# A pooling and short-convolution decoder block on one core: another step order in the first unit, a longer hold and a shorter landing count in the planner, and a rearranged closing normalisation

## The chip, the cores and the metric

The kernel runs on one core of one Trainium2 chip. The metric is the device time of one execution in microseconds (us); of the kernel before it is 2356.65 us, the median of 3 runs (2355.65 to 2356.98). TensorE (PE) multiplies, VectorE (DVE) and ScalarE (ACT) prepare its operands and take its results, SyncE (SP) and GpSimd (POOL) mostly issue DMAs.

## What is computed

One decoder block on x of shape (256, 4096), float32:

```python
h = rmsnorm(x, norm_w)
u_p, z_p, u_c, b_c, c_c, z_c, g = split(h @ w_in)      # six of width 2048, one of 8192
y_pool = pool(u_p) * silu(z_p)                         # pool: trailing windows, then a small linear map
y_conv = b_c * conv3(c_c * u_c) * silu(z_c)
merged = sigmoid(g_0 + gate_b_0) * (y_pool @ w_branch_0) + sigmoid(g_1 + gate_b_1) * (y_conv @ w_branch_1)
out = rmsnorm(x + merged @ w_out, final_norm_w)
```

The weights w_in (4096 x 20480), w_branch (2 x 2048 x 4096) and w_out (4096 x 4096) are read once each.

## The kernel before, in words

**Units and steps.** The output columns of all products are cut into units of 1024 (`cz0`, `cb0`, ... for w_in, `b0_0` to `b1_3` for w_branch, `o0` to `o3` for w_out). A unit runs through the rows of its weight in steps of 256 rows (16 steps, 8 for a branch), and a step reads one slab of weights of 1 MB into one of three buffers `raw`. A plain step ("P") makes 8 groups of 3 matmuls, since each float32 product is made of three: high times high, high times low and low times high, where "high" is the value rounded to the multiplier's format and "low" the remainder. A step of kind "S" needs only 7 groups (Strassen's scheme), but sums of quarters of both operands.

**Preparation.** For a step ACT rounds the weights (`highs`, line 231) and DVE subtracts (`lows`, line 235); both write into the 15 cells of `ring`, 4 cells for a P step, 7 for an S step. PE gives a cell back after its last product with it, and only then can another step be prepared in it. The left operands (x, later y and merged) stand in `arena` as pairs of high and low.

**The order of work is made at build time.** `pump` (line 988) lays down the preparation of the steps up to four ahead, and issues the load of step j+3 when step j is prepared; `after_group` (line 1032) is called after each group of matmuls, takes the banks that are complete out of PSUM (`evacuate` on ACT) and calls `pump`, unless it is told to hold. In the closing P step of a unit it holds after the groups 3 to 6 (line 1090). Every engine then works through its list in that order.

**The first unit** (`cz0`) has to build the pairs of x while it uses them. It runs all 16 steps as P steps, in the order `FIRST` (line 35). The operands 0 to 7 are plain pairs: ACT scales x by the norm's weight into the high (`x_direct`, line 914), DVE makes the low (`x_low`, line 908). The operands 8 to 15 are "staged": later units use them in S steps, so ACT scales into the buffer `sa` (`x_scale`, line 925) and DVE makes four sums, the rounded copy and the remainder, and copies one pair more into `extra` (`x_sums`, line 931). The staged operand of step j is laid down behind the lows of step j-1. At steps 4, 7, 10 and 13 rows of x are fetched, and at steps 6, 9, 12 and 15 they are squared for the first norm, one half on ACT and one on DVE (lines 887 to 890). The preparation of steps 0 and 1 is made in four pieces, that of the others in one; `halved` steps (line 855) are made in two.

**Fills** (class `Fill`, line 782) refresh the pairs in `arena` for later products: the planner counts ticks, one for every 6 matmuls, and lets a fill go on `LANDING` = 12 ticks after its DMA was issued (line 816). The fills of `merged` (`m_d`) belong to unit `o0`, four operands for each chunk c of 1024 columns.

**The end.** In the last unit, `o3`, three P steps are kept back and run by halves: first both column halves of the token rows 0 to 127 (t = 0), then for t = 1 one column half after the other. After each half `finish_half` (line 1175) adds the bank to `E` on DVE, squares it on ACT with a row sum into `ossq`, and multiplies it by the norm's weight on DVE. `finish` (line 1182) makes the reciprocal root of the mean (`rstd_of`, line 875: a reduction, a scale, the root on ACT, a reciprocal and three small products on DVE), scales four blocks of 128 x 1024 (one on ACT, three on DVE) and writes them out with one DMA each, the ACT block from ACT's queue and the others from SP's.

Of the kernel before, what the change touches and what calls it, by code (L numbers as in the profile page):

```python
# [15 lines left out]
P = 128  # L16
# [15 lines left out]
TAIL = 3  # L32

SIX5 = "PPPPPSPSPSPSPSPS"
FIRST = (0, 1, 8, 2, 9, 3, 10, 11, 4, 12, 13, 5, 14, 6, 15, 7)
OPENED = 12
SEVEN3 = "PPPSPSPSPSPSPSPS"
NINE = "PSPSPSPSSPSPSSPS"
# [12 lines left out]
def hybrid_block(ctx: ExitStack, tc: tile.TileContext, x, xc, prm, rows_in, w_in, pool_w, w_branch, w_out, out):  # L51
# [5 lines left out]
    def act(dst, src, func=AF.Copy, **kw):  # L57
        return pin(nc.scalar.activation(dst, src, func, **kw))  # L58
# [116 lines left out]
    class Operand:  # L175

        def __init__(self, kind, region):
            self.o, room = place(region)
            n = 4 if kind == "P" else room
            self.kind, self.region, self.n = kind, region, n  # L180
            self.ready = False
# [598 lines left out]
        o.ready = True  # L780

    class Fill:
        def __init__(self, o, src, free, ready):
            self.o, self.free, self.ready, self.src = o, free, ready, src
            self.at = self.st = None
            self.phase = self.due = 0

# [25 lines left out]
    def pop_fill(force=None):  # L813
        now[0] += 1
        for f in list(fills):
            if f.at is not None and f.free() and (now[0] >= f.at + LANDING or f.o is force):
                if f.advance(f.o is force):
                    break
        used = [f.st for f in fills if f.at is not None]
        nxt = next((f for f in fills if f.at is None), None)  # L820
        if nxt is None or not nxt.ready() or now[0] < hush[0]:
            return
        st = next((q for q in stages if not any(q is u for u in used)), None)
        if st is not None:
            nxt.fetch(st)
# [27 lines left out]
    steps = [s for u in units for s in u.steps]  # L853
    for a, b in zip(steps, steps[1:]):
        b.halved = a.kind == "S" and b.kind == "P"
    last = units[-1]
    assert all(s.kind == "P" for s in last.steps[-TAIL:])
    tail = last.steps[-TAIL:]
# [13 lines left out]
    for _ in range(WARM):  # L872
        pin(nc.tensor.matmul(shared(3)[:, 0:2 * P], warm[:, 0:P], warm, start=True, stop=True))

    def rstd_of(q, r, name):
        a = q.shape[1]
        m = sb(f"{name}_m", [P, a])
        s = sb(f"{name}_s", [P, a])
        pin(nc.vector.tensor_reduce(out=m, in_=q, axis=mybir.AxisListType.X, op=ALU.add))
        pin(nc.vector.tensor_scalar(out=m, in0=m, scalar1=1.0 / D, scalar2=EPS, op0=ALU.mult, op1=ALU.add))  # L880
        act(s, m, AF.Sqrt)
        pin(nc.vector.reciprocal(out=r, in_=s))
        mul(m, m, r)
        stt(m, m, -0.5, r, ALU.mult, ALU.mult)
        stt(r, m, 1.5, r, ALU.add, ALU.mult)
# [179 lines left out]
    def queue_fills():  # L1065
        for n in range(2):
            for i in [s.op for s in names[f"b{n}_0"].main]:
                j = y_ops[n].index(i)
                fills.append(Fill(i, y_d[n, j // 4][:, j % 4].rearrange("p k t -> p (k t)"), freed(i),
                                  lambda: True))  # L1070
# [104 lines left out]
    def finish_half(t, n):  # L1175
        cs = slice(n * NH, (n + 1) * NH)
        add(E[:, t, cs], PE_[t][n], E[:, t, cs])
        act(sa[:, 4 * n:4 * n + 4].rearrange("p o c -> p (o c)"), E[:, t, cs], AF.Square,
            accum_out=ossq[:, t, 3 + n:4 + n])
        mul(rest[:, t, cs], E[:, t, cs], Y[:, 0, cs])  # L1180

    def finish(t):
        r = rout[:, t:t + 1]
        rstd_of(ossq[:, t:t + 1], r, f"rout{t}")
        for c in range(4):
            v = rest[:, t] if c == 3 else parked[c][:, t]
            if c == 1:
                act(v, v, scale=r)
            else:
                pin(nc.vector.tensor_scalar(out=v, in0=v, scalar1=r, scalar2=None, op0=ALU.mult))  # L1190
        for c in (1, 0, 2, 3):
            v = rest[:, t] if c == 3 else parked[c][:, t]
            queue_ = nc.scalar if c == 1 else nc.sync
            pin(queue_.dma_start(of[t * P:(t + 1) * P, c * NU:(c + 1) * NU], v))

    for t in range(2):
        for ns in ((0, 1),) if t == 0 else ((0,), (1,)):
# [49 lines left out]
```

## Time and profile before

| what | before |
|---|---|
| median of 3 runs | 2356.65 us (2355.65 to 2356.98) |
| profiled execution | 2356.82 us, of which the span is 2354.7 us |
| PE busy | 2340.7 us, 10424 matmuls |
| weight loads of PE busy | 1938.7 us |
| DVE busy | 2217.8 us |
| ACT busy | 1542.9 us |
| POOL busy | 139.0 us |
| HBM read, written | 521.46 MB, 25.17 MB |

The span runs from the first to the last instruction; the rest of the execution's time lies around it. "Busy" is a share of the span. In the rows, "L61" is line 61 of the kernel, the helper that all two-operand DVE operations go through, so the tiles' names tell the operations apart: `ring<-raw,ring` are lows, `ring<-raw` on ACT are highs, `arena<-Y,par` are plain pairs of x, `sa` is the staging buffer. A row of a timeline has the start, the time, the engine, the operation and its count, and in brackets how long the engine was idle before it and what ended the wait.

### The profile page before, as it was taken

What the parts mean: (1) busy time and instruction counts of PE and PEld (TensorE: products, weight loads), DVE (VectorE), ACT (ScalarE), POOL (GpSimd) and SP (SyncE); (2) the same over time, 40 slices, a digit from 0 to 9 for tenths busy, and PEclk for the clock granted to TensorE, in tenths of its full rate; (3) what the DMA queues carried; (4) which work ended last, traced back from release to release, by engine and by line L of the source; (5) the groups of instructions that cost most, each with busy time, mean ns of one, the idle gap of its engine ahead of it and who ended that gap; (6) DMA issues with size and microseconds to landing.
All of it is one profiled execution on the core that took longest, in us unless ns stands there. A gap on an engine that the chain in (4) does not pass through costs nothing.

```text
span 2354.7 us, 28337 instructions
## 1 busy us (share of the span) xinstructions
PE 2340.7 (99%) x10424; PEld 1938.7 (82%) x10424; DVE 2217.8 (94%) x2454; ACT 1542.9 (66%) x1841; POOL 139.0 (6%) x195
## 2 busy tenths in 40 slices
PE   9999999999999999999999999999999999999998
PEld 7888888888888888888888888888888888888886
DVE  8899989999979979979999999998999899999998
ACT  6666756766656666666677767677666566566664
POOL 0000000000001000100000000001101001000000
PEclk9999999999999999999999999999999999999999
DMA  9667655776656656656787787778767678767877
GB/s 351 231 234 248 217 201 215 251 232 233 222 207 216 219 196 213 220 198 222 242 258 254 256 265 246 250 267 283 258 225 247 254 247 282 250 206 263 260 255 279
DMA packets 95387, 569.44 MB, mean 242 GB/s; under 512 B 10320, under 2 KB 10576, under 8 KB 34832
## 3 DMA queue, kind: packets, MB, share of 16 engines
q1 hardware_dynamic: 69824, 485.39, 56.7%
q0 software_dynamic: 24848, 81.01, 13.7%
q8 instruction: 81, 1.33, 0.2%
q10 hardware_dynamic: 576, 1.24, 0.1%
q14 instruction: 58, 0.48, 0.1%
HBM read 521.46 MB, written 25.17 MB: 232 GB/s over the span
## 4 chain that ended last, share of the span: by engine, by line
PE 97%; DVE 1%; DMA 0%; ACT 0%; issue 0%; DVEq 0%; SPq 0%; ACTq 0%
PE sums L1026 70%; PE shared L1026 25%; PE shared L676 1%; PE shared L462 1%; DVE ring L61 1%; DMA raw<-in_w_branch_dram 0%; DVE parts L61 0%; DMA raw<-in_w_in_dram 0%; ACT ring L58 0%; DVE arena L61 0%; PE shared L652 0%; DVE J L61 0%; ACT E L58 0%; PE shared L653 0%; PE shared L655 0%
## 5 line engine op out<-in xcount | busy, mean ns | idle before, releaser
L1026 PE MATMUL sums<-ring,arena 128*128 128x512 f32 x7011 | 1640.7, 390 | 1.9 <-ACT E L58 1.1
L1026 PEld LDWEIGHTS sums<-ring,arena 128*128 128x128 f32 x7011 | 1315.3, 188 | 275.5 <-ACT E L58 1.5
L61 DVE TENSOR_TENSOR ring<-raw,ring 128x1024 fp32r<-128x1024 f32 (+2 forms) x887 | 962.2, 1104 | 70.4 <-ACT ring L58 69.5
L58 ACT ACTIVATE ring<-raw 128x1024 fp32r<-128x1024 f32 (+3 forms) x682 | 785.5, 1192 | 210.2 <-PE sums L1026 98.5
L58 ACT ACTIVATE ring<-parts 128x512 fp32r<-128x512 f32 (+1 forms) x683 | 510.4, 761 | 510.2 <-DVE parts L61 438.3
L1026 PE MATMUL shared<-ring,arena 128*128 128x512 f32 x2241 | 541.1, 389 | 0.0
L61 DVE TENSOR_TENSOR ring<-parts,ring 128x1024 fp32r<-128x1024 f32 (+1 forms) x475 | 524.5, 1146 | 8.7 <-ACT ring L58 8.7
L1026 PEld LDWEIGHTS shared<-ring,arena 128*128 128x128 f32 x2241 | 420.6, 188 | 87.3
L61 DVE TENSOR_TENSOR parts<-parts,raw 128x512 f32<-128x512 f32 x444 | 303.3, 683 | 0.0
L61 DVE TENSOR_TENSOR parts<-raw 128x1024 f32<-128x1024 f32 x222 | 270.2, 1217 | 10.9 <-DMA raw<-in_w_in_dram 6.0
L61 DVE TENSOR_TENSOR J<-J 128x512 f32<-128x512 f32 (+1 forms) x90 | 78.1, 868 | 6.0 <-ACT J L58 2.8
L1026 PE MATMUL sums<-ring,last_pair 128*128 128x512 f32 x306 | 76.2, 389 | 0.0
L58 ACT ACTIVATE J<-shared 128x512 f32<-128x512 f32 x128 | 69.5, 601 | 1.6
L1026 PEld LDWEIGHTS sums<-ring,last_pair 128*128 128x128 f32 x306 | 57.4, 188 | 11.9
L85 POOL DMA_DIRECT2D E<-J x28 | 34.2, 1463 | 479.5 <-ACT ring L58 300.1
L1026 PE MATMUL shared<-ring,last_pair 128*128 128x512 f32 x216 | 51.9, 389 | 0.0
L1026 PE MATMUL shared<-ring,side 128*128 128x512 f32 x207 | 50.7, 389 | 0.0
L1026 PEld LDWEIGHTS shared<-ring,last_pair 128*128 128x128 f32 x216 | 40.5, 188 | 8.4
L1026 PEld LDWEIGHTS shared<-ring,side 128*128 128x128 f32 x207 | 38.9, 188 | 8.1
L58 ACT ACTIVATE E<-sums 128x512 f32<-128x512 f32 x76 | 41.8, 592 | 4.5 <-PE sums L1026 2.7
L85 POOL DMA_DIRECT2D Y<-J x12 | 14.7, 1458 | 265.1 <-ACT ring L58 138.5
L58 ACT ACTIVATE E<-sums,rin 128x512 f32<-128x512 f32 x20 | 13.0, 689 | 13.9 <-PE sums L1026 13.9
(140 smaller groups left out, 645.6 us busy)
## 6 DMA issues: line engine op xcount, KB each, us to landing
raw<-in_w_in_dram SPq DMA_DIRECT2D x318, 1024.0 KB, 4.9
raw<-in_w_branch_dram SPq DMA_DIRECT2D x64, 1024.0 KB, 5.4
raw<-in_w_out_dram SPq DMA_DIRECT2D x64, 1024.0 KB, 4.8
E<-J POOLq DMA_DIRECT2D x28, 512.0 KB, 8.6
E<-in_rows_dram POOLq DMA_DIRECT2D x14, 512.0 KB, 9.8
Y<-J POOLq DMA_DIRECT2D x12, 512.0 KB, 9.3
gates_d<-E POOLq DMA_DIRECT2D x6, 1024.0 KB, 6.1
y_d<-E POOLq DMA_DIRECT2D x8, 512.0 KB, 5.2
```

Of the source, the lines that this page charges most:

```text
L58: return pin(nc.scalar.activation(dst, src, func, **kw))
L61: return pin(nc.vector.tensor_tensor(out=dst, in0=a, in1=b, op=op))
L85: return pin(nc.gpsimd.dma_start(dst, src, accum_op=ALU.add))
L462: pin(nc.tensor.transpose(shared(j)[:, i * T + t * P:i * T + (t + 1) * P], src[:, t, c:c + P], ident))
L676: pin(nc.tensor.matmul(o, a, b, start=(k, i) == (0, 0), stop=(k, i) == (3, 2)))
L1026: pin(nc.tensor.matmul(ps, lhs, rhs, start=n == 0, stop=n == u.total[b] - 1))
```

## The change

Six edits, none of which changes a matmul or the number of matmuls:

```diff
-FIRST = (0, 1, 8, 2, 9, 3, 10, 11, 4, 12, 13, 5, 14, 6, 15, 7)
+FIRST = (0, 1, 2, 3, 8, 4, 9, 5, 10, 11, 12, 13, 14, 6, 15, 7)
...
+    for s in steps[2:5]:
+        s.halved = True
...
-            if f.at is not None and f.free() and (now[0] >= f.at + LANDING or f.o is force):
+            if f.at is not None and f.free() and (now[0] >= f.at + f.landing or f.o is force):
...
-                              lambda c=c: c in merged and now[0] >= merged[c]))
+                              lambda c=c: c in merged and now[0] >= merged[c], LANDING // (1 + c // 3)))
...
-            after_group(u, g[0], st, st is u.steps[-1] and st.kind == "P" and 3 <= i < len(gs) - 1)
+            after_group(u, g[0], st, st is u.steps[-1] and st.kind == "P" and (0 if u is names["b0_0"] else 3) <= i < len(gs) - 1)
...
+    def mean_of(q, m):
+        pin(nc.vector.tensor_reduce(out=m, in_=q, axis=mybir.AxisListType.X, op=ALU.add))
+        pin(nc.vector.tensor_scalar(out=m, in0=m, scalar1=1.0 / D, scalar2=EPS, op0=ALU.mult, op1=ALU.add))
...
+        if n == 0:
+            mean_of(ossq[:, t:t + 1, 0:4], known[:, t:t + 1])
         mul(rest[:, t, cs], E[:, t, cs], Y[:, 0, cs])
...
     def finish(t):
-        r = rout[:, t:t + 1]
-        rstd_of(ossq[:, t:t + 1], r, f"rout{t}")
-        for c in range(4):
-            v = rest[:, t] if c == 3 else parked[c][:, t]
+        r, last_, k = rout[:, t:t + 1], ossq[:, t, 4:5], known[:, t:t + 1]
+        act(dev[:, t:t + 1], last_, AF.Sqrt, scale=1.0 / D, bias=k)
+        stt(mean[:, t:t + 1], last_, 1.0 / D, k, ALU.mult, ALU.add)
+        refined(mean[:, t:t + 1], dev[:, t:t + 1], r)
+        pieces = []
+        for c, a, n in ((0, 0, NH), (1, 0, NH), (0, NH, NH), (1, NH, NH), (2, 0, NU), (3, 0, NU)):
+            v = (rest[:, t] if c == 3 else parked[c][:, t])[:, a:a + n]
             if c == 1:
                 act(v, v, scale=r)
             else:
                 pin(nc.vector.tensor_scalar(out=v, in0=v, scalar1=r, scalar2=None, op0=ALU.mult))
-        for c in (1, 0, 2, 3):
-            v = rest[:, t] if c == 3 else parked[c][:, t]
+            pieces.append((c, a, n, v))
+        for c, a, n, v in pieces:
             queue_ = nc.scalar if c == 1 else nc.sync
-            pin(queue_.dma_start(of[t * P:(t + 1) * P, c * NU:(c + 1) * NU], v))
+            pin(queue_.dma_start(of[t * P:(t + 1) * P, c * NU + a:c * NU + a + n], v))
```

In words: the first unit takes the plain operands 0 to 3 first and has five staged ones in a row at steps 8 to 12; its steps 2 to 4 are prepared in two halves. In the closing step of `b0_0` the planner lays down no preparation between any of the groups. The last four fills of `merged` (c = 3) wait 6 ticks instead of 12. At the end, the mean over the first four row sums is taken when the first half is squared, the root takes the last sum as a term of its own, and the first two blocks are scaled and written in halves.

Three places of the built program, as the engines' lists stand. First DVE in the first unit, from the lows of step 1 on (`ring<-raw,ring`), with the low of a plain pair (`arena<-Y,par,arena`, line 73) and the making of a staged operand (the rows with `sa`). Before:

```order
L61 TENSOR_TENSOR ring<-raw,ring 128x512 x4
L61 TENSOR_TENSOR sa<-sa 128x128 x4
L774 CAST arena<-sa 128x896
L61 TENSOR_TENSOR arena<-sa,arena 128x896
L774 CAST extra<-sa 128x128
L61 TENSOR_TENSOR extra<-sa,extra 128x128
L61 TENSOR_TENSOR ring<-raw,ring 128x4x512
L73 SCALAR_TENSOR_TENSOR arena<-Y,par,arena 128x256 x2
L61 TENSOR_TENSOR ring<-raw,ring 128x3x512
L61 TENSOR_TENSOR ring<-raw,ring 128x512
```

The same stretch of DVE's list in the change:

```order
L61 TENSOR_TENSOR ring<-raw,ring 128x512 x4
L73 SCALAR_TENSOR_TENSOR arena<-Y,par,arena 128x256 x2
L61 TENSOR_TENSOR ring<-raw,ring 128x2x512 x2
L73 SCALAR_TENSOR_TENSOR arena<-Y,par,arena 128x256 x2
L61 TENSOR_TENSOR ring<-raw,ring 128x2x512
L61 TENSOR_TENSOR ring<-raw,ring 128x512 x2
L61 TENSOR_TENSOR sa<-sa 128x128 x4
L774 CAST arena<-sa 128x896
L61 TENSOR_TENSOR arena<-sa,arena 128x896
L774 CAST extra<-sa 128x128
L61 TENSOR_TENSOR extra<-sa,extra 128x128
L61 TENSOR_TENSOR ring<-raw,ring 128x2x512 x2
```

The staged operand 8 has moved behind the lows of the steps 2 and 3, and plain pairs stand in its place.

Second DVE at the end of the program, from the adding of the first half of t = 1 (`sums_83` is its bank, `sums_84` that of the second half; the products into `parts` are those with the norm's weight). Before:

```order
L61 TENSOR_TENSOR E<-sums_83,E 128x512
L61 TENSOR_TENSOR parts<-E,Y 128x512
L61 TENSOR_TENSOR E<-sums_84,E 128x512
L61 TENSOR_TENSOR parts<-E,Y 128x512
L879 TENSOR_REDUCE rout_m<-ossq 128x1
L880 TENSOR_SCALAR rout_m<-rout_m 128x1
L882 RECIPROCAL rout<-rout_s 128x1
L61 TENSOR_TENSOR rout_m<-rout_m,rout 128x1
L73 SCALAR_TENSOR_TENSOR rout_m<-rout_m,rout 128x1
L73 SCALAR_TENSOR_TENSOR rout<-rout_m,rout 128x1
L1190 TENSOR_SCALAR raw<-raw,rout 128x1024 x2
L1190 TENSOR_SCALAR parts<-parts,rout 128x1024
```

The same place of DVE's list in the change:

```order
L61 TENSOR_TENSOR E<-sums_83,E 128x512
L878 TENSOR_REDUCE rout_k<-ossq 128x1
L879 TENSOR_SCALAR rout_k<-rout_k 128x1
L61 TENSOR_TENSOR parts<-E,Y 128x512
L61 TENSOR_TENSOR E<-sums_84,E 128x512
L61 TENSOR_TENSOR parts<-E,Y 128x512
L73 SCALAR_TENSOR_TENSOR rout_m<-ossq,rout_k 128x1
L890 RECIPROCAL rout<-rout_s 128x1
L61 TENSOR_TENSOR rout_m<-rout_m,rout 128x1
L73 SCALAR_TENSOR_TENSOR rout_m<-rout_m,rout 128x1
L73 SCALAR_TENSOR_TENSOR rout<-rout_m,rout 128x1
L1205 TENSOR_SCALAR raw<-raw,rout 128x512 x2
```

The reduction and its scale stand behind the first add now, ahead of the product with the norm's weight; they read `ossq`, which ACT writes from that add. The same two rows stand at that place for t = 0. Behind these rows follow one scale of `raw` (128x1024) and one of `parts` in the change.

Third ACT at the end of `b0_0`, where it copies the corner banks (`J<-shared`), rounds the next unit's weights (`ring<-raw`), makes the high of a fill (`arena<-sb`) and takes out the four product banks (`E<-sums`). Before:

```order
L58 ACTIVATE J<-shared_88 128x512
L58 ACTIVATE ring<-raw 128x3x512
L58 ACTIVATE arena<-sb 128x512
L58 ACTIVATE E<-sums_82 128x512
L58 ACTIVATE E<-sums_84 128x512
L58 ACTIVATE E<-sums_81 128x512
L58 ACTIVATE E<-sums_83 128x512
```

In the change ACT's list has the same rows in the same order at this place, and so have the other engines' lists; nothing moved there.

More of the change, by code (lines that the diff above doesn't have):

```diff
@@ L782, in hybrid_block, with __init__ @@
     class Fill:
-        def __init__(self, o, src, free, ready):
-            self.o, self.free, self.ready, self.src = o, free, ready, src
+        def __init__(self, o, src, free, ready, landing):
+            self.o, self.free, self.ready, self.src, self.landing = o, free, ready, src, landing
             self.at = self.st = None
@@ L878, in rstd_of, with refined @@
         s = sb(f"{name}_s", [P, a])
-        pin(nc.vector.tensor_reduce(out=m, in_=q, axis=mybir.AxisListType.X, op=ALU.add))
-        pin(nc.vector.tensor_scalar(out=m, in0=m, scalar1=1.0 / D, scalar2=EPS, op0=ALU.mult, op1=ALU.add))
+        mean_of(q, m)
         act(s, m, AF.Sqrt)
+        refined(m, s, r)
+    def refined(m, s, r):
         pin(nc.vector.reciprocal(out=r, in_=s))
@@ L1069, in queue_fills @@
                 fills.append(Fill(i, y_d[n, j // 4][:, j % 4].rearrange("p k t -> p (k t)"), freed(i),
-                                  lambda: True))
+                                  lambda: True, LANDING))
         for o in [s.op for s in names["o0"].main]:
@@ L1179, in finish_half @@
             accum_out=ossq[:, t, 3 + n:4 + n])
+        if n == 0:
+            mean_of(ossq[:, t:t + 1, 0:4], known[:, t:t + 1])
         mul(rest[:, t, cs], E[:, t, cs], Y[:, 0, cs])
+    known, mean, dev = (sb(f"rout_{k}", [P, 2]) for k in "kms")
     def finish(t):
-        r = rout[:, t:t + 1]
-        rstd_of(ossq[:, t:t + 1], r, f"rout{t}")
-        for c in range(4):
-            v = rest[:, t] if c == 3 else parked[c][:, t]
+        r, last_, k = rout[:, t:t + 1], ossq[:, t, 4:5], known[:, t:t + 1]
[5 more added lines that the diff above has]
+            v = (rest[:, t] if c == 3 else parked[c][:, t])[:, a:a + n]
             if c == 1:
```

## The prediction

> **What bounds the kernel now.** I start with the page: the span, the busy shares and the chain that ended last.
>
> ```profile
> span 2354.7 us, 28337 instructions
> PE 2340.7 (99%) x10424; PEld 1938.7 (82%) x10424; DVE 2217.8 (94%) x2454; ACT 1542.9 (66%) x1841; POOL 139.0 (6%) x195
> PE 97%; DVE 1%; DMA 0%; ACT 0%; issue 0%; DVEq 0%; SPq 0%; ACTq 0%
> ```
>
> PE is busy for all but 14 us, and its matmuls are the chain. The change leaves every matmul in place, so it can only touch those 14 us, or add to them. Next come the waits of PE, and two pieces of the chain in order of time.
>
> ```profile
> PE shared L873 <- DVE warm L869: 1.1, 1, 1.1
> PE sums L1026 <- ACT E L58: 1.1, 1, 1.1
> PE sums L1026 <- DVE ring L774: 0.8, 1, 0.8
> 5.98 96.11 PE sums L1026 x414
> 2326.72 17.01 PE sums L1026 x75
> ```
>
> Three waits are listed: two before the first real matmul at 5.98, which the change does not touch, and one of 1.1 us on an eviction of ACT. The last row gives 17.01 / 75 = 0.227 us for one matmul, so a P step of 24 takes 5.44 us. The 414 matmuls from 5.98 on take 96.11 us; at 0.227 they would take 94.0, and the 2.1 us more are a slow start (below). Hence there is no room in the first unit behind its start: step j begins at about 13.3 + 5.44 (j - 1). The rest of the 14 us is the end, from the last matmul to 2354.7, about 11 us.
>
> **The first unit: order and halves.** Price: nothing. The rows of before, in the timeline:
>
> ```profile
> 10.33 2.50 DVE L61 TENSOR_TENSOR ring<-raw,ring 128x512 fp32r<-128x512 f32 x4
> 14.50 1.92 ACT L58 ACTIVATE ring<-raw 128x2048 fp32r<-128x2048 f32 x1 [1.50 <-DMA raw<-in_w_in_dram]
> 16.45 2.29 DVE L61 TENSOR_TENSOR ring<-raw,ring 128x2048 fp32r<-128x2048 f32 x1
> 17.65 2.01 ACT L58 ACTIVATE ring<-raw 128x1536 fp32r<-128x1536 f32 x2 [0.44 <-DMA raw<-in_w_in_dram]
> 18.66 0.87 DVE L73 SCALAR_TENSOR_TENSOR arena<-Y,par,arena 128x256 fp32r<-128x256 f32 x2
> 30.10 1.01 DVE L61 TENSOR_TENSOR sa<-sa 128x128 f32<-128x128 f32 x4
> 33.29 1.22 DVE L73 SCALAR_TENSOR_TENSOR E<-E 128x1024 f32<-128x1024 f32 x1
> 64.04 1.92 ACT L58 ACTIVATE ring<-raw 128x2048 fp32r<-128x2048 f32 x1 [2.72 <-PE sums L1026]
> ```
>
> Step 2 (lows at 16.45) is ready at 18.74, and PE comes to it at 18.7: the only tie in the unit, and one that cost nothing. At 64.04 it is ACT that waits for PE to give cells back, so preparation is ahead there. DVE's prices: lows 2.29, a plain low 0.87, a staged operand 33.29 - 30.10 = 3.19, a square 1.2. I carry DVE's list along with them, in the new order. The lows of step 1 end at 12.83, as before. Step 2: the weights are there at 14.50, the highs come in halves of about 0.96 at 15.5 and 16.4, the plain low fits into the wait, and the lows end at 16.7 and 17.85, 0.9 before PE. Step 3: weights at 17.65, lows end at 21.2 (PE 24.2). Step 4: 3.19 of staging and 2.3 of lows, 26.7 (29.6). Steps 5 to 8 end at 29.8, 36.4, 39.6 and 45.1 (PE 35.1, 40.5, 45.9, 51.4). Then the five staged steps in a row, 8 to 12: DVE needs 5 x (3.19 + 2.29) + 2 x 1.2 = 29.8 us for what PE does in 27.2, so the lead falls from 6.3 to 3.5 us at step 12 (ready 69.6, PE 73.1), and grows again. PE never waits: **zero**. The cover is this lead; without it the run costs PE 29.8 - 27.2 = 2.6 us. Below zero there is nothing to gain, as PE has no gap here. The loads keep their order in SP's queue and are issued when the steps are prepared, within about 3 us of before.
>
> **The hold in the closing step of b0_0.** This is the wait of 1.1 us:
>
> ```profile
> 1715.76 1.49 ACT L58 ACTIVATE ring<-raw 128x1536 fp32r<-128x1536 f32 x1 [1.29 <-DMA raw<-in_w_branch_dram]
> 1717.15 0.61 ACT L58 ACTIVATE arena<-sb 128x512 fp32r<-128x512 f32 x1
> 1717.67 2.04 ACT L58 ACTIVATE E<-sums 128x512 f32<-128x512 f32 x4
> 1718.30 6.00 PE L1026 MATMUL sums<-ring,arena 128*128 128x512 f32 x25 [1.07 <-ACT E L58]
> ```
>
> ACT stands behind a load that lands at 1715.76, then rounds three cells and a fill, and only at 1717.67 takes out the first bank, which PE waits for until 1718.30. To gain, the rounding would have to move behind the evictions. The order of ACT shows that it does not: the rows are the same, since that preparation was laid down before the closing step began. So the hold costs and brings **nothing**; if it did what it says, the 1.1 us would go.
>
> **The fills of c = 3.** They move one pair of steps ahead, about 10 us:
>
> ```profile
> 2041.97 0.56 POOL L82 DMA_DIRECT2D sa<-m_d  x1 [4.57 <-DVE parts L61]
> sa<-m_d POOLq DMA_DIRECT2D x8, 256.0 KB, 5.2
> 2052.40 1.49 ACT L58 ACTIVATE ring<-raw 128x1536 fp32r<-128x1536 f32 x1 [3.00 <-PE sums L1026]
> 2061.41 1.02 DVE L61 TENSOR_TENSOR sa<-sa 128x128 f32<-128x128 f32 x4
> ```
>
> The DMA of the first is issued at 2041.97 and lands some 5 us later, at 2047; its sums now stand at 2051.2 instead of 2061.4, so the data is there. Two sums (2.0 us) come ahead of a preparation in whose course ACT waits 3.0 us for PE at 2052.40; DVE's delay of at most 2 to 3 us is inside a lead of a like size, and PE has no wait there to give back: **zero**, at worst some 0.5 us.
>
> **The end.** Here stands the one term that isn't zero. The rows of before:
>
> ```profile
> 2335.60 0.69 DVE L61 TENSOR_TENSOR E<-sums,E 128x512 f32<-128x512 f32 x1 [1.05 <-PE sums L1026]
> 2336.32 0.63 ACT L58 ACTIVATE sa<-E 128x512 f32<-128x512 f32 x1 [7.01 <-DVE E L61]
> 2336.86 0.19 ACT L58 ACTIVATION_READ_ACCUMULATOR sa<-E 128x1 f32 x1
> 2338.41 0.16 DVE L879 TENSOR_REDUCE rout_m<-ossq 128x1 f32<-128x5 f32 x1
> 2339.80 1.42 DVE L1190 TENSOR_SCALAR raw<-raw,rout 128x1024 f32<-128x1024 f32 x2
> 2341.80 0.68 DVE L61 TENSOR_TENSOR E<-sums,E 128x512 f32<-128x512 f32 x1
> 2343.76 0.69 DVE L61 TENSOR_TENSOR E<-sums,E 128x512 f32<-128x512 f32 x1 [0.55 <-PE sums L1026]
> 2345.24 0.16 DVE L879 TENSOR_REDUCE rout_m<-ossq 128x1 f32<-128x5 f32 x1
> 2345.85 0.16 DVE L882 RECIPROCAL rout<-rout_s 128x1 f32<-128x1 f32 x1 [0.27 <-ACT rout_s L58]
> 2346.63 1.42 DVE L1190 TENSOR_SCALAR raw<-raw,rout 128x1024 f32<-128x1024 f32 x2
> 2347.41 0.99 SPq L1194 DMA_DIRECT2D out_dram<-raw  x2
> DMA packets 506, 1.88 MB, mean 417 GB/s; under 512 B 48, under 2 KB 48, under 8 KB 506
> DMA packets 986, 1.36 MB, mean 272 GB/s; under 512 B 233, under 2 KB 469, under 8 KB 986
> ```
>
> The row with 417 GB/s is the stretch 2348.5 to 2353.0: the writes of t = 1 run at one rate from the first DMA (issued 2347.41) to the end, 2.10 MB / 417 = 5.0 us. So **the issue of the first DMA sets the end**. What must be late for it? The first half of t = 1 was complete in PSUM at about 2339.5, but DVE adds it only at 2341.80: DVE is behind, with the scales of t = 0. Then it waits 0.55 us for PE and adds the second half at 2343.76.
>
> The edit shortens the chain behind the second square: the reduction and its scale go (2345.24 to 2345.62, 0.38 us), and the first scale is half as long (about 0.36 for 0.71). But it puts the reduction behind the *first* add, where DVE, whose list is in order, must wait for ACT's square. For t = 0: the add ends at 2336.29, square and sum end at 2337.05, reduction and scale take until 2337.42; the product starts at 2337.44 instead of 2336.32. The second add moves from 2336.93 to 2338.05, the second square ends at 2339.50, the root at 2339.71, the reciprocal starts at 2339.74 and the first scale 0.78 later (2346.63 - 2345.85), at 2340.52 against 2339.80. The four scales are followed by the first add of t = 1 at 2342.54 against 2341.80. There the same wait comes once more: square done at 2343.99, reduction and scale until 2344.36, product, and the second add starts at 2344.99, although its bank was complete at 2343.7. Square done 2346.44, root 2346.65, reciprocal 2346.68, first scale 2347.46 against 2346.63. Its half ends 0.36 later, and the first DMA goes at 2347.90 against 2347.41: **0.5 us later**. Behind it the halves follow each 0.36, and 256 KB take 0.63 us at 417 GB/s, so the writes do not starve.
>
> The halves have rows of 2 KB in place of 4 KB. The trace has no such write. Its nearest rows are loads with 2 KB rows in the first 7 us, a mean of 272 GB/s (last row, the stretch 2 to 7) with pauses; by that the 1.05 MB in halves would take 3.9 us for 2.5, 1.3 more; at 417 GB/s, nothing. I take 0.15, near the lower end, since the slow start of the program is in the 272.
>
> Sum: 0 + 0 + 0 + 0.5 + 0.15 = +0.65 us against the profiled execution, 2356.82 (span 2354.7 and 2.1 around it), 2357.47. The median lies 0.17 below that execution, so I forecast 2357.3 us. Ends: -0.75 (both savings at the end arrive, no backlog) and +1.8 (halves at 272 GB/s).
>
> **The rivals.** *The end is faster.* If DVE were not behind, or the waits for the squares cost it less, the savings of 0.38 and 0.36 remain: 2355.9. For it speaks the shorter chain, against it the add at 2341.80, 2.3 us after its bank. A further 1.1 us would go if the load at 1715.76 landed earlier by chance: 2354.8. *The hold or the order bring more*, over 0.2%: that needs 4.7 us out of the 14, of which 6 lie before the first matmul and 5 are writes; I see no place.
>
> *Slower: the five staged steps starve PE.* The place is step 12, the price 2.6 us if the lead at step 8 is zero instead of 6.3; it decides from a lead under 2.6. A stop of that length could also throw PE back to its slow start, which cost 2.1 us (the 96.11 row). With the end that is 2356.65 + 0.65 + 2.6 + 2.1 = 2362.0. Against it speaks the row at 64.04, where ACT waits for PE.
>
> The wait at 1718.30 bears on the second part of this price: 1.07 us of idle PE, and the 25 matmuls behind it take 6.00 us, 0.24 each, so PE stayed fast. [...]
>
> *The change does nothing at the end either* (the waits and the savings cancel): 2356.6.
>
> **How the numbers follow.** About 0.2% (4.7 us) is what a measurement of this kernel can tell from no change. Forecast, the end later by 0.2 to 1.8 us: 0.62. End unchanged or faster: 0.26. A small starvation of PE, under 4 us: 0.06. The starvation with a slow restart: 0.04. Faster by over 0.2%, for a reason not seen: 0.02. So faster 0.02, same 0.94, slower 0.04. The range takes both ends of the term and what lies in the run of before: 2355.0 to 2359.2.
>
> **What would show it.** In the changed profile PE's waits should again be one on the warm-up, one on `ring` and one of about 1.1 us on `E`; a fourth on `ring` or `arena` between 60 and 80 us would be the starvation. The reduction should stand 0.8 us after the add that it follows, idle for ACT's `sa`, and the second add of t = 1 near 2345.0, without a wait for PE; if it waits for PE again, the backlog was misread and the end is faster. The first write of t = 1 should be issued near 2347.9 and the writes fill 5.0 to 5.3 us.

## The result and the profile after

The changed kernel took **2360.45 us**, the median of 20 runs (2359.53 to 2362.82), against 2356.74 us for 20 runs of the kernel before in the same series (2355.65 to 2359.19). The ratio is 1.0016, with a 95% interval of 1.001 to 1.0023. The forecast was 2357.3 with a range up to 2359.2: the sign was right, the time lies above the range. On the two profiled executions the spans are 2358.7 and 2354.7 us, 4.0 apart.

The page of the changed kernel, span and busy shares:

```profile
span 2358.7 us, 28360 instructions
PE 2344.0 (99%) x10424; PEld 1938.6 (82%) x10424; DVE 2218.6 (94%) x2461; ACT 1544.3 (65%) x1846; POOL 139.0 (6%) x195
```

PE is 3.3 us busier with the same 10424 matmuls. No case of the prediction had that. Its list of waits, which was the first thing to look at by the prediction, is the same as before, with one of them shorter (the columns are the sum, the number and the longest, in us):

```profile
PE shared L875 <- DVE warm L871: 1.1, 1, 1.1
PE sums L1034 <- DVE ring L774: 0.8, 1, 0.8
PE sums L1034 <- ACT E L58: 0.7, 1, 0.7
```

So PE lost its 3.3 us without waiting for anyone: its matmuls themselves are longer. The view that groups PE's instructions by line and tiles says which. Before:

```profile
L1026 PE MATMUL shared<-ring,arena 128*128 128x512 f32 x2241 | 541.1, 389 | 0.0
L1026 PE MATMUL sums<-ring,last_pair 128*128 128x512 f32 x306 | 76.2, 389 | 0.0
L1026 PE MATMUL shared<-ring,last_pair 128*128 128x512 f32 x216 | 51.9, 389 | 0.0
```

The changed kernel, in the same view:

```profile
L1034 PE MATMUL shared<-ring,arena 128*128 128x512 f32 x2241 | 541.1, 389 | 0.0
L1034 PE MATMUL sums<-ring,last_pair 128*128 128x512 f32 x306 | 78.1, 395 | 0.0
L1034 PE MATMUL shared<-ring,last_pair 128*128 128x512 f32 x216 | 53.3, 396 | 0.0
```

Of each row the busy time (in us) and the mean of one (in ns) matter. Matmuls overlap, so the mean of 389 ns, from a matmul's start to its end, is longer than the distance from one start to the next, which is 226.7 ns by the start times. Only the 522 matmuls whose pair comes from `last_pair` have changed: 395 and 396 ns, 233 ns from start to start. They cost (78.1 + 53.3) - (76.2 + 51.9) = **3.3 us** more. Those on `arena` are as before.

The other part is the end. The timeline of the changed kernel from the last matmuls to the first writes:

```profile
2345.09 1.56 PE L1034 MATMUL sums<-ring,last_pair 128*128 128x512 f32 x6
2345.48 0.68 DVE L61 TENSOR_TENSOR E<-sums,E 128x512 f32<-128x512 f32 x1
2346.95 0.16 DVE L878 TENSOR_REDUCE rout_k<-ossq 128x1 f32<-128x4 f32 x1 [0.79 <-ACT sa L58]
2347.82 0.68 DVE L61 TENSOR_TENSOR E<-sums,E 128x512 f32<-128x512 f32 x1
2350.39 1.54 DVE L1205 TENSOR_SCALAR raw<-raw,rout 128x512 f32<-128x512 f32 x3
2350.91 1.39 SPq L1209 DMA_DIRECT2D out_dram<-raw  x3
```

The rows stand where the prediction put them relative to the last matmul: the reduction idles 0.79 us for ACT's `sa`, and the second add comes without a wait for PE. The last matmul ends at 2345.09 + 1.56 = 2346.65, the first write is issued at 2350.91, and the span ends at 2358.7. Set against the last matmul of before, whose row is this,

```profile
2342.20 1.52 PE L1026 MATMUL sums<-ring,last_pair 128*128 128x512 f32 x6
```

the stretches are (times in us; three further kernels of the experiments stand beside them):

| kernel | last matmul to first write | first write to end | together |
|---|---|---|---|
| before | 2343.72 to 2347.41: 3.69 | 7.29 | 10.98 |
| changed | 2346.65 to 2350.91: 4.26 | 7.79 | 12.05 |
| e1, changed kernel at the addresses of before | 2344.55 to 2348.90: 4.35 | 7.60 | 11.95 |
| e12, whole blocks | 2341.70 to 2346.20: 4.50 | 7.30 | 11.80 |
| e7, reduction later | 2341.22 to 2344.38: 3.16 | 7.62 | 10.78 |

The end has cost 1.07 us. The third difference is the wait in the closing step of `b0_0`, 0.71 for 1.07 us. Together 3.3 + 1.07 - 0.36 = 4.0 us, which is the difference of the spans.

### The profile page after: what moved, and what is told of

Its sections match the earlier page's. It is cut to its first block, busy times and chain, and to the rows that moved or that the text cites. A ratio compares the mean times of both kernels' runs of the same rounds, so it can differ in the third digit from the quotient of the medians.

```text
span 2358.7 us, 28360 instructions
## 1 busy us (share of the span) xinstructions
PE 2344.0 (99%) x10424; PEld 1938.6 (82%) x10424; DVE 2218.6 (94%) x2461; ACT 1544.3 (65%) x1846; POOL 139.0 (6%) x195
## 4 chain that ended last, share of the span: by engine, by line
PE 97%; DVE 2%; ACT 0%; DMA 0%; issue 0%; DVEq 0%; SPq 0%; ACTq 0%
PE sums L1034 70%; PE shared L1034 25%; PE shared L676 1%; PE shared L462 1%; DVE ring L61 1%; DMA raw<-in_w_branch_dram 0%; DVE parts L61 0%; ACT ring L58 0%; DMA raw<-in_w_in_dram 0%; DVE arena L61 0%; ACT sa L58 0%; DVE raw L1205 0%; PE shared L652 0%; DVE J L61 0%; DVE E L61 0%
## 5 line engine op out<-in xcount | busy, mean ns | idle before, releaser
L1034 PE MATMUL sums<-ring,arena 128*128 128x512 f32 x7011 | 1640.7, 390 | 1.5 <-DVE ring L774 0.8
L61 DVE TENSOR_TENSOR J<-J 128x512 f32<-128x512 f32 (+1 forms) x90 | 78.1, 868 | 6.3 <-ACT J L58 2.8
L1034 PE MATMUL sums<-ring,last_pair 128*128 128x512 f32 x306 | 78.1, 395 | 0.0
L1034 PE MATMUL shared<-ring,last_pair 128*128 128x512 f32 x216 | 53.3, 396 | 0.0
```

The source lines that it names most:

```text
L61: return pin(nc.vector.tensor_tensor(out=dst, in0=a, in1=b, op=op))
L1034: pin(nc.tensor.matmul(ps, lhs, rhs, start=n == 0, stop=n == u.total[b] - 1))
```

## The experiments

The theory after these traces: six edits that touch no matmul have shifted a tile. The changed kernel keeps three small tiles of [128, 2] (`known`, `mean`, `dev`) where before had four of [128, 1] (two each for t = 0 and t = 1). By the addresses of the built program a tile of either kind takes 32 bytes of each partition, so the pool that holds them is one tile smaller, and `last_pair`, which stands behind it, starts at byte 187424 instead of 187392. `raw`, from which most of the output is written at the end, moves by 32 bytes too, from 195584 to 195616. In the kernel before, all tiles that feed those products start at multiples of 512: `arena` 2560, `ring` 88576, `extra` 171008, `side` 179200, `last_pair` 187392. The rival: the end, the order of the first unit or the small tiles themselves make the difference, and the longer matmuls come with them. In the diffs below, `front` and `back` are tiles that nothing uses; `back` has 40 columns of 4 bytes in both kernels.

**The address alone, from both sides: e1 and e2.** e1 is the changed kernel with its tiles back at the addresses of before.

```diff
-    sb("back", [P, 40])
+    sb("back", [P, 48])
```

> The kernel after, with 32 bytes more of filling in the upper part of the memory, so that every tile there has the address of before (last_pair at 187392 instead of 187424). Nothing else is changed. Theory P (place): the matmuls with last_pair as stationary operand take 6.3 ns more each because the tile starts 32 bytes further on; expected is a pitch of 226.7 ns for them, PE busy 2340.7 us, and 2357.3 us (before 2356.7, plus 1.1 for the end, less 0.4 at the eviction of b0_0). Rival Q (order): the pitch rises because the changed order of the lists lets ACT or DVE touch last_pair or raw at the same time; expected is then still 233 ns and 2360.4 us.

e2 is the kernel before with `last_pair` and `raw` at the addresses of the changed one.

```diff
-    sb("back", [P, 40])
+    sb("back", [P, 32])
```

> The kernel before, with 32 bytes less of filling: the tiles of the upper part start 32 bytes further on, last_pair at 187424. No instruction moves. Theory P: 233 ns for the 521 matmuls with last_pair, PE busy 2344.0 us, 2359.5 us (3.3 us more, of which the waits at b0_0 and in o2 take back 0.4 to 0.6). Rival Q: no change, 2356.7 us.

Measured: e1 2356.66 us, ratio to before 0.9997 (0.9988 to 1.0006); e2 2361.26, ratio 1.0018 (1.0009 to 1.0026), beside 2357.03 for before. PE's group in e1, then in e2:

```profile
L1034 PE MATMUL sums<-ring,last_pair 128*128 128x512 f32 x306 | 76.2, 389 | 0.0
```

```profile
L1026 PE MATMUL sums<-ring,last_pair 128*128 128x512 f32 x306 | 78.1, 395 | 0.0
```

Eight unused columns take the whole loss away from the changed kernel, and eight fewer put 4.2 us on the kernel before, where nothing else was touched. The address is the main cause. The medians give it 3.8 and 4.2 us, more than the 3.3 of the matmuls, and e2 is 1.8 above its expectation. In the traces of before and e2 the last matmul comes 4.3 us later: 3.3 of that in the matmuls on `last_pair`, 0.2 in a later first product, 0.6 among those on `arena`, waits included. The writes of the end, too, take about 0.1 us longer with `raw` 32 or 64 bytes further on: 7.38 us from the first write to the end in e2 and 7.41 in e5, against 7.27 to 7.30 in before, e10, e11 and e12, which write whole blocks with `raw` at the address of before. The rest I can't put down to the address.

**Which distance: e4, e6, e5, e13, e14.** Is it the tile's own address, or its place against the other operand? e4 moves `ring`, the moving operand of nearly all matmuls, and the tiles behind it by 32 bytes, `last_pair` too, but not `arena`:

```diff
+    blocks("gap", [P, 8])
     ring = blocks("ring", [P, CELLS, 2, NH], F32R)
...
-    sb("back", [P, 40])
+    sb("back", [P, 32])
```

> The kernel before with 32 bytes between arena and ring, and 32 bytes less of filling above: arena stays, ring, extra, side and last_pair start 32 bytes further on. If only the stationary operand's place counts: extra (36), side (276) and last_pair (521) take 6.3 ns more each, 5.2 us, 2361.9 us; the matmuls with arena keep 227 ns although their moving operand, ring, has moved. If the moving operand's place counts as well, all 10000 take 6 ns more, some 60 us, 2417 us.

e6 moves all of them by 32 bytes:

```diff
-    blocks("front", [P, 96])
+    blocks("front", [P, 104])
...
-    sb("back", [P, 40])
+    sb("back", [P, 32])
```

> The kernel before with all tiles that feed PE (arena, ring, extra, side, last_pair) started 32 bytes further on. Theory M (mismatch): a matmul is slow when its stationary and its moving operand stand 32 bytes apart modulo 64, so with both moved alike all have 227 ns again: 2356.7 us. Rival A (absolute place): a moving operand that doesn't start on a multiple of 64 bytes is slow by itself; then all take 233 ns, as in the run with ring moved alone: 2417 us.

Measured: e4 **2417.24 us**, ratio 1.0255 (1.0236 to 1.0274); e6 2357.28, ratio 1.0 (0.999 to 1.001). The groups of e4, and below them those of e6:

```profile
L1027 PE MATMUL shared<-ring,arena 128*128 128x512 f32 x2241 | 555.9, 395 | 0.0
L1027 PE MATMUL sums<-ring,last_pair 128*128 128x512 f32 x306 | 76.6, 390 | 0.0
```

```profile
L1026 PE MATMUL shared<-ring,arena 128*128 128x512 f32 x2241 | 541.1, 389 | 0.0
L1026 PE MATMUL sums<-ring,last_pair 128*128 128x512 f32 x306 | 76.2, 389 | 0.0
```

In e4 the slow and the quick group have changed places: `arena` is at 233.3 ns from start to start, `last_pair` at 226.8 to 227.5. Some 9250 matmuls at 6.5 ns more are 60 us, and that is the measured difference. In e6 nothing is slow, though none of these tiles stands at a multiple of 64 any more. By these two runs what counts is how the two operands stand to each other.

The other three ask for the period. e5 moves `last_pair` by 64 bytes (`back` [P, 24]), e13 moves all the others by 128 (`front` [P, 64]), e14 by 256 (`front` [P, 32]), each in the kernel before.

> The kernel before with the upper tiles started 64 bytes further on, last_pair at 187456. Theory M (mismatch modulo 64): 64 bytes are no mismatch, 227 ns for the matmuls with last_pair. Rival: any move away from the multiple of 512 of before costs, 233 ns.

> The kernel before with arena, ring, extra and side started 128 bytes earlier, last_pair left where it was: the two sides stand 128 bytes apart modulo 512. If the mismatch counts modulo 128, all matmuls keep 227 ns and the time is that of before, 2356.9 us. If it counts modulo 256 or 512, the 521 matmuls with last_pair take 233 ns, 2360 us, and the others 227.

> The same with 256 bytes. Modulo 128 or 256: 227 ns for all, 2356.9 us. Modulo 512: 233 ns for the matmuls with last_pair, 2360 us.

Measured: 2361.18, 2359.54 and 2359.45 us, one run each. The group of 306 on `last_pair` in e5, in e13 and in e14:

```profile
L1026 PE MATMUL sums<-ring,last_pair 128*128 128x512 f32 x306 | 78.2, 396 | 0.0
```

```profile
L1026 PE MATMUL sums<-ring,last_pair 128*128 128x512 f32 x306 | 77.8, 394 | 0.0
```

```profile
L1026 PE MATMUL sums<-ring,last_pair 128*128 128x512 f32 x306 | 76.2, 389 | 0.0
```

64 bytes cost as much as 32 (233.5 ns from start to start), 128 nearly so (232.6), and 256 nothing (226.7). My theory that 64 bytes apart would be free fell with e5; a period of 256 bytes fits all of these kernels (distances of 0, 32, 64, 128 and 256 bytes beyond a multiple of 512). The time of e14 is not that of its matmuls on `last_pair`: its one run had a stop of 2.2 us in `b0_0` and a drop of the clock behind it (its 7011 matmuls of `sums` on `arena` take 1641.8 us in all, those of before 1640.7), of which more below. Why 256, no run here shows.

**What the other edits are worth: e3.** The changed kernel at the addresses of before, with the order, the halves, the landing count and the hold undone, so that only the new end is left:

```diff
-FIRST = (0, 1, 2, 3, 8, 4, 9, 5, 10, 11, 12, 13, 14, 6, 15, 7)
+FIRST = (0, 1, 8, 2, 9, 3, 10, 11, 4, 12, 13, 5, 14, 6, 15, 7)
...
-    for s in steps[2:5]:
-        s.halved = True
...
```

> The end of the kernel after alone: order of the first unit, halves, landing and hold are those of before, and the filling keeps all addresses of before. Theory P: the other edits are worth nothing, so it is as long as e1: 2357.8 us, with the first write of t = 1 about 4.6 us after the last matmul (4.1 before) and 1.1 us more from there and in the writes together. Rival: the first unit's order or the fills carry a part of the 3.7 us; then e1 and e3 differ by more than 0.6 us.

Measured: 2358.71 us, ratio 1.0007 (0.9998 to 1.0016). That is 1.7 above before, and 2.05 above e1: the undone edits are worth some 2 us, which I had put at nothing, and 8 of e1's 11 runs lie below the lowest of e3. PE's beginning in e3 (old order):

```profile
5.94 11.54 PE L1032 MATMUL sums<-ring,arena 128*128 128x512 f32 x49 [0.80 <-DVE ring L774]
19.31 5.04 PE L1032 MATMUL sums<-ring,arena 128*128 128x512 f32 x14 [1.82 <-DVE ring L61]
```

The same place in e1 (new order):

```profile
5.83 11.43 PE L1034 MATMUL sums<-ring,arena 128*128 128x512 f32 x49 [0.95 <-DVE ring L774]
17.78 14.37 PE L1034 MATMUL sums<-ring,arena 128*128 128x512 f32 x62 [0.52 <-DVE ring L61]
```

Both reach step 2 after 49 matmuls, e3 at 17.48 and not at 18.7 as in the profile of before: in this execution PE did not begin slowly. The stretches 6 to 10 and 19.5 to 23 show it (length, then PE, its weight loads, DVE, ACT and POOL busy with counts, the granted clock, DMA share, GB/s). Before:

```profile
6.00:10.00 4.00, 4.00 (x10) 3.13 (x11) 3.74 (x8) 3.11 (x7) 0.00 (x0) 1.00 1.03 368
19.50:23.00 3.50, 3.50 (x17) 2.92 (x16) 3.43 (x8) 3.20 (x6) 0.00 (x0) 1.00 0.99 372
```

The same stretches of e3:

```profile
6.00:10.00 4.00, 4.00 (x18) 3.08 (x19) 3.20 (x7) 2.61 (x6) 0.00 (x0) 1.00 0.95 337
19.50:23.00 3.50, 3.50 (x9) 2.73 (x10) 3.47 (x8) 3.14 (x5) 0.00 (x0) 0.53 0.98 363
```

PE does 10 matmuls from 6 to 10 in one execution and 18 in the other. In e3, where PE begins quickly, the old order makes it wait 1.82 us for the lows of step 2, and then the clock falls to 0.53, so that 14 matmuls take 5.04 us, 0.36 each, 1.9 us more than at 0.227 (1.7 by the start times). In e1, with the new order, the wait is 0.52 us and the clock stays up (1.00 from 19.5 to 23). In the slow beginning both orders nearly fit (with the old order PE waits for nothing at step 2 in before and e2, 0.2 us in e14 and 0.4 in e6), and that was the beginning of the one execution that I had read.

**The order by itself, and with a longer warm-up: e8, e10, e11.** e8 is the kernel before with the new order and the halves of steps 2 to 4.

> The kernel before with the new order of the first unit and its three steps in halves, nothing else. Theory S (step 2): in runs where PE's clock is up at its first product, PE reaches step 2 two us earlier; the order of before then makes it wait 2 us there, and the clock falls for another 2 us, while the new order waits 0.7 us. Expected: 1 to 2 us less than before, 2355.5 us, and a profile with no wait over 1 us near 17. Rival Z: the edit is worth nothing, 2356.9 us, as was forecast.

Measured: 2356.12 us, ratio 0.9994 (0.9985 to 1.0003). Its profiled execution began slowly, with 10 matmuls from 6 to 10, and has no wait at step 2. With the same 18 warm-up matmuls before and the changed kernel began slowly too (10 and 11), e1 and e3 quickly (18 each). A program that begins quickly more often should show the order better, hence e10, the kernel before with four more warm-up matmuls, and e11, e8 with the same:

```diff
-WARM = 18
+WARM = 22
```

> The kernel before with 22 warm-up matmuls. Theory S: PE's clock is up at the first product, PE comes to step 2 at 16.7, waits about 2 us for the lows of that step, which DVE makes in one piece, and in a part of the runs falls back to the slow clock for 2 us more: 2356.7 to 2359 us, no faster than before. Rival W: the warm-up is worth 2 us by itself, 2354.8 us.

> The same 22 warm-up matmuls with the new order of the first unit and its halves, all else as before. Theory S: the wait at step 2 is 0.7 us and the clock stays up, 1.3 us less than before in every run: 2355.5 us, and 1.5 to 3 us less than the run with the order of before. Rival Z (the order is worth nothing): equal to that run.

Measured: e10 2357.22 us, ratio 1.0001 (0.9992 to 1.001), e11 2355.27, ratio 0.9993 (0.9984 to 1.0002). Both intervals hold 1, but 8 of e11's 11 runs lie below the lowest of e10, and the medians are 1.95 us apart, as e1 and e3 are. Both profiled executions began quickly (16 and 17 matmuls from 6 to 10). Their waits at step 2, of e10 and of e11:

```profile
PE sums L1026 <- DVE ring L61: 1.2, 1, 1.2
```

```profile
PE sums L1028 <- DVE ring L61: 0.5, 1, 0.5
```

The order takes 0.7 us off the wait there. The rest of the 1.95 would be falls of the clock that it spares; that share is argued from e3's trace and not shown, since neither of these two traces has such a fall.

**The end, mended: e12, e7, e9.** e12 is e1 with whole blocks:

```diff
-        for c, a, n in ((0, 0, NH), (1, 0, NH), (0, NH, NH), (1, NH, NH), (2, 0, NU), (3, 0, NU)):
+        for c, a, n in ((0, 0, NU), (1, 0, NU), (2, 0, NU), (3, 0, NU)):
```

> The kernel after with the addresses of before and with the blocks of the end scaled and written whole, four DMAs a row block as before; the mean stays ahead of the product. From the last matmul to the end of the span it was 11.3 us before and 12.5 after. If the halves cost more than they bring (rows of 2 KB, two more issues), first issue 0.36 later than after (5.0 us behind the last matmul), 7.3 from there: 12.3. If they bring their 0.36: 12.8.

(The expectations of e3 and e12 count from the start of the last matmul, 0.4 us ahead of its end.) Measured: 2355.61 us in one run. Against e1, which has the same addresses, the first write comes later (4.50 us behind the last matmul instead of 4.35), but from there to the end it takes 7.30 instead of 7.60: the halves cost 0.15 us on balance. SP's queue at the writes of t = 1, first in e1, then in e12 (start, time, what it issues):

```profile
2348.90 1.39 SPq L1209 DMA_DIRECT2D out_dram<-raw  x3
2350.62 0.52 SPq L1209 DMA_DIRECT2D out_dram<-parts  x1
```

```profile
2346.20 0.99 SPq L1209 DMA_DIRECT2D out_dram<-raw  x2
2347.52 0.33 SPq L1209 DMA_DIRECT2D out_dram<-parts  x1
```

With halves the last issue ends 2.24 us after the first one's start, without them 1.65. Of these 0.59 us, 0.40 are a later start behind an earlier first issue, and 0.19 a longer issue. The three on `raw` are two halves and one whole block; a half took SP 0.33 to 0.42 us to issue in the changed kernel, no less than a whole block (0.33 in before), so the halves add issues and make none shorter. Which of this makes the 0.30 us behind the first issue, the rows don't decide.

The rate in the writes fell in the changed kernel, from 417 GB/s in the stretch that the prediction showed to 396 from 2352 to 2356.5, while e12 from 2347 to 2351.5 stays at 418:

```profile
DMA packets 748, 1.78 MB, mean 396 GB/s; under 512 B 80, under 2 KB 80, under 8 KB 748
```

```profile
DMA packets 507, 1.88 MB, mean 418 GB/s; under 512 B 48, under 2 KB 48, under 8 KB 507
```

But little of that is the halves: e1, with the same halves and `raw` at the address of before, writes at 414 GB/s from 2350 to 2354.5. e2, with whole blocks and `raw` 32 bytes further on, writes at 403 from 2352.8 to 2357.3:

```profile
DMA packets 491, 1.81 MB, mean 403 GB/s; under 512 B 48, under 2 KB 48, under 8 KB 491
```

So of the 0.50 us that the changed kernel's writes take longer than before (7.79 for 7.29), 0.3 go with the halves (7.60 in e1), and the other 0.2 with the address.

e7 is e1 with three repairs: the reduction behind the product, so that DVE does not idle for ACT's square; one halved block instead of two; and a hold in `b0_0` that begins in the step before, where the preparation in question is laid down.

```diff
+        mul(rest[:, t, cs], E[:, t, cs], Y[:, 0, cs])
         if n == 0:
             mean_of(ossq[:, t:t + 1, 0:4], known[:, t:t + 1])
-        mul(rest[:, t, cs], E[:, t, cs], Y[:, 0, cs])
...
-        for c, a, n in ((0, 0, NH), (1, 0, NH), (0, NH, NH), (1, NH, NH), (2, 0, NU), (3, 0, NU)):
+        for c, a, n in ((0, 0, NH), (1, 0, NU), (0, NH, NH), (2, 0, NU), (3, 0, NU)):
...
+                        or u is names["b0_0"] and st is u.steps[-2] and i >= 5)
...
-            pump()
+            if not (u is names["b0_0"] and st is u.steps[-2]):
+                pump()
```

> The kernel after with the addresses of before, the mean laid down behind the product with the norm's weight instead of ahead of it, only the first block in halves, and the hold begun in the step before the closing one, so that ACT rounds the next unit's weights behind the four evictions. Expected: no wait of PE on E near 1716 (1.1 us less than before), the first write of t = 1 0.6 us sooner than before: 2355.3 us, and 2354.3 if the new order of the first unit brings 1 us. Rival: if the evictions wait for something else than the list of ACT, 2356.4 us.

Measured: 2355.24 us, ratio 0.9995 (0.9986 to 1.0004); span 2352.0. Its end:

```profile
2341.03 0.16 DVE L878 TENSOR_REDUCE rout_k<-ossq 128x1 f32<-128x4 f32 x1
2341.29 0.68 DVE L61 TENSOR_TENSOR E<-sums,E 128x512 f32<-128x512 f32 x1
2344.38 1.39 SPq L1211 DMA_DIRECT2D out_dram<-raw  x3
```

The reduction no longer idles, the second add comes 0.26 us behind its start instead of 0.87, and the first write 3.16 us behind the last matmul: the shorter chain does save 0.5 us against before once DVE's list lets it. Its one halved block takes back 0.3 of that (7.62 for 7.29). And ACT and PE at the end of `b0_0`:

```profile
1713.47 2.64 ACT L58 ACTIVATE E<-sums 128x512 f32<-128x512 f32 x4 [0.22 <-PE sums L1034]
1716.01 1.48 ACT L58 ACTIVATE ring<-raw 128x1536 fp32r<-128x1536 f32 x1
1709.65 10.59 PE L1034 MATMUL sums<-ring,arena 128*128 128x512 f32 x46
```

The evictions stand ahead of the rounding now, and PE goes through without a wait. But a wait of 0.7 us on ACT's `E` is in its list, at 1756, the end of `b1_0`, where before has none. e9 and e2 have one of 0.8 there, and they too have none in `b0_0`, so most of the wait moved, and the repair is worth some 0.3 us. Two of e7's eleven runs took 2359.6 and 2359.8, and no trace says why. e9 is e7 with `WARM = 22`:

> The mended kernel with 22 warm-up matmuls in place of 18, so that PE is busy until 5.8 us. Theory S: the clock is up at the first product in every run; the ten slow matmuls go (2.0 us) and a wait of 0.7 us at step 2 comes: 1.3 us less than the mended kernel where that starts slowly, and runs closer together: 2354.0 us. Rival: the state of the clock at the start hangs on the moment and not on the warm-up, then it is as long as the mended kernel.

Measured: **2354.61 us** (2354.02 to 2356.45), ratio 0.999 (0.9981 to 0.9999): below both kernels, though by little.

## Why the prediction was wrong, point by point

- **The step that failed:** "The change leaves every matmul in place, so it can only touch those 14 us, or add to them." The matmuls stayed in place, but their duration was taken as fixed. A tile fewer moved `last_pair` by 32 bytes against `ring`, and 522 matmuls became 6.3 ns longer each: 3.3 us, the larger part of the loss, shown by e1 and e2 in both directions. The sum had no term for it. No rival had it, since none asked what stands where in the memory. The rows to see it in beforehand were not in the trace; the diff names the new tiles (`known`, `mean`, `dev`), and the program's addresses tell the shift. (Of the 14 us themselves only 1.9 lie ahead of the first product, as the two waits there show, and not the 6 of the rivals; the rest of the 6 is warm-up, which counts as busy. No term of the sum hung on that.)
- **The end:** the mechanism was right, add by add, and so was the first term: +0.5 forecast, +0.57 measured. The second was mis-sized: the halves were put at 0.15, and the writes took 0.50 more (7.79 for 7.29), 0.3 of it with the halves (e1) and 0.2 with `raw`'s new address. Sum 1.07 for 0.65.
- **The first unit:** "Below zero there is nothing to gain, as PE has no gap here" was read from one execution with a slow beginning. In those that begin quickly with the old order PE has a gap there, 1.2 to 1.8 us at step 2 (e3, e4, e5, e10, e13), and the new order takes most of it away, about 2 us by the medians (e1 against e3, e11 against e10), 0.7 without the longer warm-up (e8). The point that the five staged steps starve nothing was right: no wait of PE between 60 and 80 us.
- **The slow restart:** its price of 2.1 us, taken from the row of 96.11, was right in size (1.9 in e3), but the place was another. The longest stop that the prediction could read, 1.07 us with PE fast behind it, did not tell what a longer one does: the clock fell behind 1.82 us of idle PE in e3, and behind 1.98 us in `b0_0` of e1. PE's timeline of e1 there:

```profile
1717.96 1.65 PE L1034 MATMUL sums<-ring,arena 128*128 128x512 f32 x3 [1.98 <-ACT E L58]
```

  and the stretch behind it, with 11 matmuls in 4 us at a granted clock of 0.58:

```profile
1718.00:1722.00 4.00, 4.00 (x11) 3.20 (x12) 4.00 (x7) 3.43 (x6) 0.00 (x0) 0.58 0.38 150
```

  The length of the stop is not all of it, since e5 idled 1.82 us at step 2 as well and kept its clock. In these traces the changes of the clock lie whole multiples of 3.413 us apart: at 10.25 and 2348.38 in before (685 steps), at 9.50 and 2351.04 in the changed kernel (686 steps), at 5.75, 19.41 and 22.82 in e3, at 4.46, 1717.95 and 1721.37 in e1. Here is e3 cut along these times, and below it e5 along its own (counted from 4.47):

```profile
15.99:19.41 3.42, 1.60 (x8) 0.95 (x6) 3.19 (x5) 3.04 (x4) 0.00 (x0) 1.00 1.02 424
19.41:22.82 3.41, 3.41 (x8) 2.65 (x9) 3.38 (x7) 3.05 (x5) 0.00 (x0) 0.50 0.96 356
```

```profile
14.71:18.12 3.41, 2.70 (x12) 1.88 (x10) 3.10 (x5) 2.74 (x4) 0.00 (x0) 1.00 1.04 423
18.12:21.54 3.42, 2.31 (x10) 1.95 (x11) 3.42 (x4) 2.99 (x5) 0.00 (x0) 1.00 1.00 382
```

  e3's stop lies in one stretch, in which PE was busy for 1.60 us, and the clock is at half for exactly the next one. e5's stop is shared between two, with PE busy for 2.70 and 2.31 us.

- **The hold** changed no instruction's place and no cause of the wait, as forecast. That the wait is 0.71 us in the changed kernel and 1.98 in e1, with the same order, comes from the load that ACT stands behind: it idles 0.93 us for it in the one and 2.18 in the other.

```profile
1718.33 1.49 ACT L58 ACTIVATE ring<-raw 128x1536 fp32r<-128x1536 f32 x1 [0.93 <-DMA raw<-in_w_branch_dram]
```

```profile
1715.41 1.48 ACT L58 ACTIVATE ring<-raw 128x1536 fp32r<-128x1536 f32 x1 [2.18 <-DMA raw<-in_w_branch_dram]
```

- **The fills** brought no wait to PE and took none of the listed ones away, as forecast; no run had them alone.

## What to carry to other kernels

This kernel is bound by one engine at 99%, and its instructions' own durations were the largest term: a shift of 32 bytes made 522 matmuls 3.3 us longer (the changed kernel) and some 9250 of them 60 us (e4). So where an edit adds, drops or resizes a tile, compare the addresses of the operands before and after (here 0 and 256 bytes beyond a multiple of 512 between them cost nothing, 32, 64 and 128 some 6 ns a matmul), and compare the mean of each matmul group before looking at waits. A "no gap here" that is read from one execution holds for its state of the clock alone; ask what comes late if the engine gets there 1 or 2 us sooner (17.48 for 18.7 in e3, and a wait of 1.82). A reduction that moves off the end of a chain has to go behind work that doesn't depend on it, else the engine idles for its input in the middle of the list (0.79 us in the changed kernel, nothing in e7).

## What the runs showed of the hardware

- A product of 128 x 128 by 128 x 512 in this kernel takes 226.7 ns from start to start where its stationary and its moving operand stand 0 or 256 bytes beyond a multiple of 512 apart (before, e14), 233.0 to 233.3 where it is 32 (the changed kernel, e4), 233.5 at 64 (e5) and 232.6 at 128 (e13). With some 9250 such products 32 bytes off the kernel became 2.55% slower (e4).
- PE's clock fell to half for 3.41 us, eight matmuls in e3, where PE had idled 1.82 us (e3) and 1.98 (e1) within one stretch of the 3.413 us grid of the traces; in e14 it fell behind a stop of 2.2. It did not fall behind a stop of 1.6 us (e6), nor where 1.82 us were shared between two stretches (e5, 0.71 and 1.11). That the place of the stop on the grid matters rests on e3 against e5 alone, and no run shows why.
- In the stretch from 6 to 10 us PE did 10 matmuls in before and 18 in e3, both at a granted clock shown as 1.00. The clock's record in the trace begins at 10.25 us in before and at 9.50 in the changed kernel, and the column counts the time ahead of it as full. Ahead of it the matmuls start 427 ns apart in both, behind it 227 (medians). In e3 and e1, which begin quickly, the record begins at 5.75 and 4.46.
- The DMA of a half block (128 rows of 2 KB) held SP for 0.33 to 0.42 us in the changed kernel, a whole block (rows of 4 KB) for 0.33 in before, and the whole block behind the halves for 0.52 (e1) and 0.71 (changed kernel).
- The writes of the end ran at 417 to 418 GB/s from `raw` at byte 195584 (before, e12) and at 403 from byte 195616 (e2), all in whole blocks.
